# A triangular solve beside the DeltaNet groups: issue order of its second half, and later stores of its blocks

## The chip, the cores and the metric

The kernel runs on one core of a Trainium2 chip. The metric is the device time of one execution in microseconds. Every time below is of that kind or comes from one execution taken by the hardware profiler.

## The reference

One decoder layer for 512 tokens and a model width of 2048, all in float32. Two branches work in parallel on the same normalised input, and a gated sum of both is projected and added to the residual. One branch is sliding-window attention. The other is a gated DeltaNet with 16 key heads and 32 value heads of 128 channels; the change is there. Its core, cut to what matters:

```python
# chunks of C = 64 tokens, N = 8 chunks, H = 32 heads
L = jnp.where(strict, jnp.einsum('bhncd,bhnsd->bhncs', k_beta, k) * decay, 0.0)
t_inv = lax.linalg.triangular_solve(eye + L, jnp.broadcast_to(eye, L.shape),
                                    left_side=True, lower=True, unit_diagonal=True)
u = t_inv @ v_beta
w = t_inv @ (k_beta * jnp.exp(g)[..., None])
...
def step(S, xs):
    v_new = u_c - w_c @ S
    o = qd_c @ S + qk_c @ v_new
    S = S * gl_c[..., None, None] + jnp.swapaxes(kd_c, -1, -2) @ v_new
    return S, o
```

So for each of 32 heads and 8 chunks a 64 x 64 unit lower triangular matrix is inverted, and a scan over chunks uses the inverses.

## The kernel before, in words

**The main stream.** Nearly all time goes into projections on TensorE. A `channel_tile` (L227) makes 128 output channels for all 512 tokens: 16 blocks of the contraction, each as three matmuls of 128x128 by 128x512 (L223, L224, L225), because weights and activations are split into a high and a low part (`split`, L50: ScalarE writes the high part on L52, VectorE the low part on L53). A weight tile of 1 MB is loaded by `load_job` (L183) into one of two `raw` buffers; each half of it is split into one of three pairs `whi`, `wlo`. A load is issued when the second half of an older tile has been split.

**How side work is woven in.** After every second block of the contraction, `channel_tile` calls `pump` (L81). A pump advances all generators in `live`, whose `yield n` means "go on after n pumps", and those in `slow`: `paced` (L72) gives a generator a budget per pump, and its `yield x` means that x of budget must have come together before its next step. So the text of the program, written out by the generators, is one long list in which the side work stands between matmuls. `drain_slow` (L120) writes out at once what is left of a generator. A compiler pass then orders each engine's list; what must stay behind what on one engine can be given by an edge. `with tc.issue_after(ins)` (L716) puts such edges: what the block issues on the engine of `ins` stands behind `ins` in that engine's list, without a wait for a result. `self.chain` (L64) is the last instruction of the latest `rsqrt` that has been written, that is of the latest norm on VectorE.

**The stages around the change** (`deltanet`, L571). First come the keys of 16 heads (`keys`, L624) between tiles of merge gates (`merge_gate`, L242). Each key head leaves its triangular blocks in DRAM (`lt_d`, `lab_d`) and has a norm of its own (L636). Then come 16 groups (`heads`, L740), one per key head, of five channel tiles each: a query tile (`queries`, L770), two value tiles (`values`, L759) and two gate tiles. Every query and value tile goes through a causal convolution (`conv`, L554): ScalarE evicts it (L558), VectorE adds three shifted products (L561), ScalarE takes a tanh (L566), VectorE multiplies (L568); then TensorE transposes it (ptq on L781, ptv on L765, both recorded on L257). `queries` also masks two decay matrices on GpSimd (L685, L686), takes their exponentials on ScalarE (L811), and reads the solved blocks (L802 to L807). `scan` (L850) then runs the four chunk pairs and ends in an output norm (L912 to L915), whose `rsqrt` becomes the new `self.chain`.

**The solve** (`solve`, L690). Only the 64 x 64 diagonal blocks are inverted; two solves of 16 heads each: solve 0 for the heads of groups 0 to 7, solve 1 for groups 8 to 15. One solve loads 128 matrices, one on each partition, into `A` (L699), scales them (L709), and takes 62 steps of two VectorE operations: an outer product into `atmp` (L717, m x n elements a partition, n = 63 - m) and an addition into `A` (L723). Both are inside `issue_after(self.chain.ins)`. Then ScalarE copies the first 64 matrices transposed, in four parts (L728), and each part is stored in `ta_d` (L729); VectorE scales `A` in place (L733), and two stores write `ts_d` (L736). `atmp` has one buffer.

**Their paces.** Solve 0 is begun with a budget of 0.7 a pump (L596) and gets 1.4 for the last three merge-gate tiles (L602); `drain_slow` (L606) writes what is left of it before the groups begin. Solve 1 is begun there with 0.45 (L607) and drained, if anything is left, before group 8 (L617).

Of the kernel before, what the change touches and what calls it, by code (L numbers as in the profile page):

```python
# [2 lines left out]

# [22 lines left out]
HD = 64  # L26
# [10 lines left out]
class Layer:  # L37
# [533 lines left out]
    def deltanet(self):  # L571
        tc, nc, a = self.tc, self.nc, self.a
        dram = self.dram
        self.lt_d = dram.tile([2, 2, 16, 4, HD, HD], F32, name="lt_d")
        self.lab_d = dram.tile([VH, HD, 4, HD], F32, name="lab_d")
        self.ta_d = dram.tile([2, 16, 4, HD, HD], F32, name="ta_d")
        self.ts_d = dram.tile([2, 2, 16, 4, HD, HD], F32, name="ts_d")
        self.kT_d = dram.tile([KH, P, T], F32, name="kT_d")
        self.k_d = dram.tile([KH, P, T], F32, name="k_d")
        self.o_d = dram.tile([VH, P, T], F32, name="o_d")  # L580
        with ExitStack() as ps:
            self.pmm = ps.enter_context(tc.tile_pool(name="pmm", bufs=2, space=PSUM, reuse_waits="tile"))
            self.ptp = ps.enter_context(tc.tile_pool(name="ptp", bufs=2, space=PSUM, reuse_waits="tile"))
            self.gwk = ps.enter_context(tc.tile_pool(name="gwk", bufs=1, reuse_waits="tile"))
            sol1 = ps.enter_context(tc.tile_pool(name="sol1", bufs=1, side="right", reuse_waits="tile"))
            with ExitStack() as sa:
                wk = sa.enter_context(tc.tile_pool(name="dnA", bufs=2, reuse_waits="tile"))
                sol0 = sa.enter_context(tc.tile_pool(name="sol0", bufs=1, reuse_waits="tile"))
                gp = sa.enter_context(tc.tile_pool(name="gates", bufs=1, reuse_waits="tile"))
                self.go(self.gates(gp), 1)  # L590
                self.keys_done = []
                for g in range(NST):
                    self.go(self.keys(wk, g, self.acc_k[g]), 10 + 8 * g)
                for j in range(NFIRST):
                    self.merge_gate("mb", j, self.mb_d)
                s0 = self.paced(self.solve(sol0, 0, nc.vector), 0.7)  # L596
                for kind, j in self.mixed():
                    if kind == "k":
                        self.go(self.keys(wk, j, self.channel_tile(f"k{j}")), 0)
                    else:  # L600
                        self.merge_gate("mb", j, self.mb_d)
                s0[1] = 1.4  # L602
                for j in range(3):
                    self.merge_gate("ma", j, self.ma_d)
                self.drain_live()
                self.drain_slow(s0)  # L606
                s1 = self.paced(self.solve(sol1, 1, nc.vector), 0.45)  # L607
            with ExitStack() as sb:
                wk = sb.enter_context(tc.tile_pool(name="dnB", bufs=2, reuse_waits="tile"))
                self.tt = []  # L610
                for n in range(4):
                    t = wk.tile([P, NTB, P], F32, tag=f"tt{n}", name=f"tt{n}", bufs=1)
                    nc.gpsimd.memset(t[HD:P, :, 0:HD], 0.0)
                    self.tt.append(t)
                for g in range(KH):
                    if g == 8:
                        self.drain_slow(s1)  # L617
                    self.heads(wk, g)
                for j in range(3, 5):
                    self.merge_gate("ma", j, self.ma_d)  # L620
                self.drain_live()
        self.dump("o", self.o_d)
# [67 lines left out]
    def solve(self, wk, b, eng):  # L690

        nc = self.nc
        while not all(g in self.keys_done for g in range(8 * b, 8 * b + 8)):
            yield 1.0
        A = wk.tile([P, HD, HD], F32, tag=f"A{b}", name="A", bufs=1)
        bet = wk.tile([P, HD], F32, tag=f"bet{b}", name="bet", bufs=1)
        for k2 in range(2):
            s = slice(k2 * HD, (k2 + 1) * HD)
            nc.sync.dma_start(  # L699
                out=A[s].rearrange("u j i -> u (j i)"), in_=self.lt_d[b, k2].rearrange("h c j i -> (h c) (j i)")  # L700
            )
            nc.sync.dma_start(
                out=bet[s],
                in_=self.b_rows.rearrange("h (c k i) -> k (h c) i", c=4, k=2)[k2, b * HD : (b + 1) * HD, :],
            )
        yield 8.0
        nb = wk.tile([P, HD], F32, tag=f"nbet{b}", name="nbet", bufs=1)
        eng.tensor_scalar(out=nb, in0=bet, scalar1=-1.0, scalar2=None, op0=ALU.mult)
        eng.tensor_tensor(out=A, in0=A, in1=nb.unsqueeze(1).to_broadcast([P, HD, HD]), op=ALU.mult)  # L709
        eng.memset(A.rearrange("u j i -> u (j i)")[:, 0 : HD * HD : HD + 1], 1.0)  # L710
        for m in range(1, HD - 1):
            n = HD - 1 - m
            yield 0.2 + 0.0023 * m * n
            tmp = wk.tile([P, 1024], F32, tag=f"atmp{b}", name="atmp", bufs=1)
            t = tmp[:, : m * n].rearrange("p (j i) -> p j i", j=m)
            with self.tc.issue_after(self.chain.ins):  # L716
                eng.tensor_tensor(  # L717
                    out=t,
                    in0=A[:, m : m + 1, m + 1 :].to_broadcast([P, m, n]),
                    in1=A[:, :m, m : m + 1].to_broadcast([P, m, n]),  # L720
                    op=ALU.mult,
                )
                eng.tensor_tensor(out=A[:, :m, m + 1 :], in0=A[:, :m, m + 1 :], in1=t, op=ALU.add)  # L723
        for q in range(4):
            yield 1.5
            tmp = wk.tile([P, 1024], F32, tag=f"atmp{b}", name="atmp", bufs=1)
            t = tmp.rearrange("p (i j) -> p i j", j=HD)[:HD]
            nc.scalar.copy(out=t, in_=A[:HD, :, q * 16 : (q + 1) * 16].rearrange("u j i -> u i j"))  # L728
            nc.sync.dma_start(  # L729
                out=self.ta_d[b].rearrange("h c i j -> (h c) (i j)")[:, q * 1024 : (q + 1) * 1024], in_=tmp[:HD]  # L730
            )
        yield 4.5
        eng.tensor_tensor(out=A, in0=A, in1=bet.unsqueeze(2).to_broadcast([P, HD, HD]), op=ALU.mult)  # L733
        for k2 in range(2):
            s = slice(k2 * HD, (k2 + 1) * HD)
            nc.sync.dma_start(  # L736
                out=self.ts_d[b, k2].rearrange("h c j i -> (h c) (j i)"), in_=A[s].rearrange("u j i -> u (j i)")
            )
# [780 lines left out]
```

## Time and profile before

| | us |
|---|---|
| median of three runs | 2983.45 |
| lowest and highest of them | 2979.93, 2987.34 |
| the profiled execution | 2983.62 |
| its span, first to last instruction | 2981.8 |

| engine in the profiled execution | busy us | share of the span |
|---|---|---|
| TensorE | 2891.9 | 97% |
| VectorE | 1790.1 | 60% |
| ScalarE | 1085.9 | 36% |
| GpSimd | 243.0 | 8% |

The mean granted TensorE clock of that execution was 0.987. In its profile, PE is TensorE's matmuls, PEld its weight loads, DVE VectorE, ACT ScalarE, POOL GpSimd, and SP the engine that issues the DMAs here. Times in the profile count from the start of the span. A row of a stretch gives its bounds and length, and then the busy time of each engine with its number of instructions. A row in order of time gives start, length, engine, line, operation, output, inputs and shape, and in brackets how long the engine sat idle before it and what ended that. A row of waits gives the waiting instruction, what it waited for, the total in us, the number of waits and the longest.

### The profile page before, as it was taken

How to read it: one execution, taken by the hardware profiler on the slowest of the kernel's cores; microseconds unless marked ns; L12 is line 12 of the kernel's file. 1: busy time of each engine (PE TensorE's matmuls, PEld its weight loads, DVE VectorE, ACT ScalarE, POOL GpSimd, SP SyncE). 2: the span in 40 equal slices, each digit the busy share in tenths (PEclk: the TensorE clock that was granted, in tenths of full speed). 3: DMA queues.
4: the chain of work that ended last, by engine and by line, in shares of the span. 5: the costliest groups of instructions: out<-in, count | busy, mean ns of one | idle time of the engine just before them, and what ended most of it. 6: DMA issues, size and time to landing. Idle time of an engine off the chain costs nothing.

```text
span 2981.8 us, 38024 instructions
## 1 busy us (share of the span) xinstructions
PE 2891.9 (97%) x14556; PEld 2367.8 (79%) x14556; DVE 1790.1 (60%) x2903; ACT 1085.9 (36%) x2105; POOL 243.0 (8%) x204
## 2 busy tenths in 40 slices
PE   8899999999999999999999999999999999999988
PEld 6687777778787788888888878888788788788877
DVE  7755979567676544545454453433756655554697
ACT  4354332433333433333433322311334444432343
POOL 0022210111111000001100000000100000000013
PEclk9999999999999999999999999999999999999999
DMA  9756545633333533334332575555322223375562
GB/s 387 269 168 182 181 136 158 180 113 121 108 107 107 147 124 119 116 116 132 117 120 100 174 265 208 186 169 165 109 87 87 89 87 102 112 258 173 177 197 96
DMA packets 174023, 451.11 MB, mean 151 GB/s; under 512 B 72177, under 2 KB 74737, under 8 KB 138129
## 3 DMA queue, kind: packets, MB, share of 16 engines
q1 hardware_dynamic: 173842, 448.70, 45.6%
q8 instruction: 114, 1.87, 0.3%
q14 instruction: 67, 0.55, 0.1%
HBM read 386.95 MB, written 59.45 MB: 150 GB/s over the span
## 4 chain that ended last, share of the span: by engine, by line
PE 78%; DVE 9%; DMA 6%; ACT 3%; issue 2%; POOL 2%; SPq 1%; POOLq 0%; DVEq 0%; ACTq 0%
PE mm L223 22%; PE mm L225 21%; PE mm L224 21%; DVE wlo L53 2%; DMA E<-g_rows 2%; DVE wa L396 1%; PE S L1159 1%; PE pv L870 1%; ACT whi L52 1%; PE po L889 1%; PE O L1210 1%; PE pP L257 1%; DMA oraw<-o_d 1%; POOL E L685 1%; PE po L888 1%
## 5 line engine op out<-in xcount | busy, mean ns | idle before, releaser
L223 PE MATMUL mm<-hh,whi 128*128 128x512 f32 x2784 | 1138.3, 409 | 4.4 <-DVE yq L561 3.6
L225 PE MATMUL mm<-hh,wlo 128*128 128x512 f32 x2784 | 1095.5, 393 | 0.0
L224 PE MATMUL mm<-hl,whi 128*128 128x512 f32 x2784 | 1093.5, 393 | 0.0
L53 DVE TENSOR_TENSOR wlo<-raw,whi 128x1024 fp32r<-128x1024 f32 (+1 forms) x452 | 551.8, 1223 | 481.2 <-ACT whi L52 470.3
L52 ACT CAST whi<-raw 128x1024 fp32r<-128x1024 f32 (+1 forms) x452 | 470.8, 1043 | 981.9 <-PE mm L224 928.3
L223 PEld LDWEIGHTS mm<-hh,whi 128*128 128x128 f32 x2784 | 528.0, 190 | 114.9 <-issue 12.4
L225 PEld LDWEIGHTS mm<-hh,wlo 128*128 128x128 f32 x2784 | 526.6, 189 | 115.2
L224 PEld LDWEIGHTS mm<-hl,whi 128*128 128x128 f32 x2784 | 528.4, 190 | 99.8 <-issue 0.4
L223 PE MATMUL mm<-oh,whi 128*128 128x512 f32 x512 | 201.3, 395 | 2.2 <-ACT oh L52 1.2
L225 PE MATMUL mm<-oh,wlo 128*128 128x512 f32 x512 | 200.1, 391 | 0.5 <-DVE wlo L53 0.5
L224 PE MATMUL mm<-ol,whi 128*128 128x512 f32 x512 | 200.0, 391 | 0.5 <-DVE ol L53 0.5
L817 POOL TENSOR_TENSOR qe<-qe,yq 128x512 f32<-128x512 f32 x32 | 49.4, 1561 | 919.9 <-DMA qe<-eg_rows 738.9
L223 PEld LDWEIGHTS mm<-oh,whi 128*128 128x128 f32 x512 | 96.4, 189 | 24.8 <-ACT oh L52 2.6
L685 POOL TENSOR_TENSOR E<-E,neg_g 128x512 f32<-128x512 f32 x64 | 74.2, 1160 | 491.9 <-DMA E<-g_rows 465.2
L224 PEld LDWEIGHTS mm<-ol,whi 128*128 128x128 f32 x512 | 96.4, 188 | 22.3 <-DVE ol L53 1.5
L225 PEld LDWEIGHTS mm<-oh,wlo 128*128 128x128 f32 x512 | 96.5, 189 | 21.2 <-DVE wlo L53 1.3
L723 DVE TENSOR_TENSOR A<-A,atmp 128x486 f32<-128x486 f32 (+30 forms) x124 | 111.5, 905 | 1.8
L717 DVE TENSOR_TENSOR atmp<-A 128x62 f32<-128x62 f32 (+30 forms) x124 | 108.7, 882 | 1.8
L863 DVE SCALAR_TENSOR_TENSOR r<-pp,neg_eg,vt 128x128 f32<-128x128 f32 x96 | 29.3, 346 | 87.7 <-PE pp L860 85.8
L561 DVE SCALAR_TENSOR_TENSOR yv<-mm,convh,yv 128x511 f32<-128x511 f32 (+2 forms) x96 | 71.1, 741 | 8.5 <-ACT yv L558 7.5
L1183 ACT ACTIVATE sm<-sm,mx,rs 128x256 f32<-128x256 f32 (+1 forms) x128 | 71.7, 561 | 3.3 <-DVE mx L1178 3.3
L224 PE MATMUL m<-wlo,hh 128*128 128x512 f32 x128 | 51.4, 402 | 9.1 <-DVE wlo L53 9.1
(331 smaller groups left out, 3161.6 us busy)
## 6 DMA issues: line engine op xcount, KB each, us to landing
raw<-in_w_ch SPq DMA_DIRECT2D x158, 1024.0 KB
wa<-in_w_ada_ss SPq DMA_DIRECT2D x32, 1024.0 KB
raw<-in_w_od SPq DMA_DIRECT2D x32, 1024.0 KB
E<-g_rows SPq DMA_DIRECT2D x64, 256.0 KB
gw<-in_w_ada_gate SPq DMA_DIRECT2D x16, 1024.0 KB
raw<-in_w_os SPq DMA_DIRECT2D x16, 1024.0 KB
qe<-eg_rows SPq DMA_DIRECT2D x32, 256.0 KB
o_d<-zh SPq DMA_DIRECT2D x32, 256.0 KB
```

The source lines that it names most:

```text
L52: self.nc.scalar.copy(out=hi, in_=src)
L53: self.nc.vector.tensor_tensor(out=lo, in0=src, in1=hi.bitcast(F32), op=ALU.subtract)
L223: nc.tensor.matmul(ps, lhsT=wh, rhs=xh, start=first, stop=False)
L224: nc.tensor.matmul(ps, lhsT=wh, rhs=xl, start=False, stop=False)
L225: nc.tensor.matmul(ps, lhsT=wl, rhs=xh, start=False, stop=last)
L257: self.nc.tensor.transpose(dst[:, c * P : (c + 1) * P], src_cols(c), self.ident)
L561: nc.vector.scalar_tensor_tensor(out=y[:, s:], in0=ps[:, : T - s], scalar=w[:, j : j + 1], in1=y[:, s:], op0=ALU.mult, op1=ALU.add)
L685: nc.gpsimd.tensor_tensor(out=E, in0=E, in1=ng, op=ALU.add)
L717: eng.tensor_tensor(out=t, in0=A[:, m : m + 1, m + 1 :].to_broadcast([P, m, n]), in1=A[:, :m, m : m + 1].to_broadcast([P, m, n]), op=ALU.mult,
L723: eng.tensor_tensor(out=A[:, :m, m + 1 :], in0=A[:, :m, m + 1 :], in1=t, op=ALU.add)
L817: nc.gpsimd.tensor_tensor(out=qf, in0=qf, in1=q, op=ALU.mult)
L1183: nc.scalar.activation(t, t, AF.Exp, scale=r[:, h : h + 1], bias=mx[:, h : h + 1], accum_out=den[:, h : h + 1])
```

## The change

Three things differ. The edge to the latest norm is put for solve 0 alone; for solve 1 `nullcontext` takes its place. In the solve's end, the stores stand some steps of the pace behind the operations that make their data: 2.5 between a copy and its store, and 8.0 between the last scaling and the `ts_d` stores, while the yield ahead of that scaling goes from 4.5 to 1.5. And the budgets are larger: 1.9 in place of 1.4 for solve 0's last part, 0.5 in place of 0.45 for solve 1. With the yields added up, a solve asks for 15 more of budget than before (126.7 to 141.7 in all).

```diff
-                s0[1] = 1.4
+                s0[1] = 1.9
                 for j in range(3):
                     self.merge_gate("ma", j, self.ma_d)
                 self.drain_live()
                 self.drain_slow(s0)
-                s1 = self.paced(self.solve(sol1, 1, nc.vector), 0.45)
+                s1 = self.paced(self.solve(sol1, 1, nc.vector), 0.5)
...
             t = tmp[:, : m * n].rearrange("p (j i) -> p j i", j=m)
-            with self.tc.issue_after(self.chain.ins):
+            with self.tc.issue_after(self.chain.ins) if b == 0 else nullcontext():
                 eng.tensor_tensor(
...
+        rows = self.ta_d[b].rearrange("h c i j -> (h c) (i j)")
         for q in range(4):
             yield 1.5
             tmp = wk.tile([P, 1024], F32, tag=f"atmp{b}", name="atmp", bufs=1)
             t = tmp.rearrange("p (i j) -> p i j", j=HD)[:HD]
             nc.scalar.copy(out=t, in_=A[:HD, :, q * 16 : (q + 1) * 16].rearrange("u j i -> u i j"))
-            nc.sync.dma_start(
-                out=self.ta_d[b].rearrange("h c i j -> (h c) (i j)")[:, q * 1024 : (q + 1) * 1024], in_=tmp[:HD]
-            )
-        yield 4.5
+            yield 2.5
+            nc.sync.dma_start(out=rows[:, q * 1024 : (q + 1) * 1024], in_=tmp[:HD])
+        yield 1.5
         eng.tensor_tensor(out=A, in0=A, in1=bet.unsqueeze(2).to_broadcast([P, HD, HD]), op=ALU.mult)
+        yield 8.0
         for k2 in range(2):
```

More of the change, by code (lines that the diff above doesn't have):

```diff
@@ L1 @@
 import math
-from contextlib import ExitStack
+from contextlib import ExitStack, nullcontext
 import concourse.bass as bass
```

## The prediction

> **What bounds the kernel now.** I read the page's first part, then busy time by stretches cut at the DeltaNet groups, then TensorE's waits in the same stretches, then the instructions around one wait, in order of time.
>
> ```profile
> span 2981.8 us, 38024 instructions
> PE 2891.9 (97%) x14556; PEld 2367.8 (79%) x14556; DVE 1790.1 (60%) x2903; ACT 1085.9 (36%) x2105; POOL 243.0 (8%) x204
> ```
>
> TensorE is busy for 97% of the span. None of its work changes, so the edit can only give or take TensorE idle time, and the half-speed clock that follows idling. The second solve runs beside the DeltaNet groups. I cut the stretches where L912 opens a group's output norm, once in every group. Columns: PE, PEld, DVE, ACT, POOL busy (instructions), granted clock, DMA share, GB/s.
>
> ```profile
> 541.00:640.70 99.70, 93.14 (x451) 76.52 (x450) 42.86 (x58) 35.81 (x65) 10.86 (x10) 0.95 0.54 154
> 640.70:711.10 70.40, 67.54 (x358) 55.99 (x357) 51.67 (x82) 25.13 (x58) 8.05 (x6) 1.00 0.36 114
> 711.10:782.60 71.50, 69.04 (x357) 57.22 (x357) 49.62 (x77) 25.01 (x56) 7.83 (x6) 0.98 0.34 112
> 782.60:854.70 72.10, 69.11 (x358) 57.24 (x357) 49.18 (x77) 25.03 (x57) 7.77 (x6) 0.98 0.34 111
> 854.70:926.30 71.60, 69.10 (x358) 57.24 (x357) 51.30 (x80) 25.04 (x57) 7.89 (x6) 0.98 0.33 109
> 926.30:998.70 72.40, 68.69 (x357) 56.94 (x356) 51.83 (x89) 24.99 (x56) 7.99 (x6) 0.98 0.34 113
> 998.70:1070.60 71.90, 69.26 (x358) 57.20 (x357) 42.25 (x73) 32.68 (x62) 7.26 (x6) 0.98 0.54 155
> 1070.60:1137.90 67.30, 67.30 (x357) 56.02 (x357) 33.49 (x64) 25.11 (x57) 6.29 (x6) 1.00 0.37 119
> ```
>
> A period without the solve takes 67.3 us with no TensorE idle (last row). The six periods with it take 70.4 to 72.4, together 1070.6 - 640.7 = 429.9. The excess is 429.9 - 6 x 67.3 = **26.1 us**, 4.35 a period. In the row 782.6, for instance, idle is 72.10 - 69.11 = 2.99 and the clock of 0.98 costs 2% of 72, 1.4: together 4.4 of its 4.8. The first row has 99.70 - 93.14 = 6.56 idle and 5% of clock, about 5.0: 11.6 us. The waits, for 641 to 1071 (first two rows) and 541 to 641 (last two):
>
> ```profile
> PE ptv L257 <- DVE yv L568: 14.8, 6, 3.7
> PE pu L835 <- DVE Y L831: 2.3, 1, 2.3
> ...
> PE mm L223 <- DVE yq L561: 3.6, 1, 3.6
> PE ptq L257 <- DVE yq L568: 2.9, 1, 2.9
> ```
>
> So there is **one wait in each group**: the transpose of a value tile (ptv) waits for that tile's last convolution step, L568. Here is its cause, first in a group with the solve and then, from 1146, in one without.
>
> ```profile
> 650.62 0.64 POOL L686 TENSOR_SCALAR_AFFINE_SELECT E<-E 128x512 f32<-128x512 f32 x1
> 651.29 0.63 ACT L811 ACTIVATE E<-E 128x512 f32<-128x512 f32 x1 [6.25 <-POOL E L686]
> 653.60 0.63 ACT L811 ACTIVATE E<-E 128x512 f32<-128x512 f32 x1 [1.68 <-POOL E L686]
> 655.07 0.62 ACT L566 ACTIVATE th<-yv 128x512 f32<-128x512 f32 x1
> ...
> 1147.17 0.63 ACT L811 ACTIVATE E<-E 128x512 f32<-128x512 f32 x1 [4.97 <-POOL E L686]
> 1147.71 0.62 ACT L566 ACTIVATE th<-yv 128x512 f32<-128x512 f32 x1
> 1148.89 0.63 ACT L811 ACTIVATE E<-E 128x512 f32<-128x512 f32 x1 [0.57 <-POOL E L686]
> ```
>
> ScalarE runs its list in order. Without the solve, the tanh L566 stands between the two exponentials L811. With it, solve steps delay the three L561 of the convolution, L566 has slipped behind the second L811, and that one waits for a late POOL mask.
>
> **The change, part by part.** First I ask where the second solve's steps run now. L717 and L723 are the two halves of a step; here are their own busy times.
>
> ```profile
> 505.00:541.00 36.00, 12.76 (x26) 1.00 0.34 118
> 541.00:640.70 99.70, 0.00 (x0) 0.95 0.54 154
> 640.70:711.10 70.40, 9.82 (x9) 1.00 0.36 114
> ...
> sum 632.90, DVE 59.07; mean DVE 6.56
> ...
> 505.00:541.00 36.00, 13.46 (x26) 1.00 0.34 118
> ...
> 640.70:711.10 70.40, 9.15 (x9) 1.00 0.36 114
> ...
> sum 632.90, DVE 62.90; mean DVE 6.99
> ```
>
> ```profile
> 539.28 0.88 DVE L717 TENSOR_TENSOR atmp<-A 128x686 f32<-128x686 f32 x1
> 561.40 0.68 ACT L558 ACTIVATE yq<-mm,convh 128x512 f32<-128x512 f32 x1
> 643.23 0.90 DVE L717 TENSOR_TENSOR atmp<-A 128x720 f32<-128x720 f32 x1
> ```
>
> Step 14 (686 elements, 14 x 49) ran at 539, before TensorE had finished even the first tile of group 0 (its eviction is the row at 561). In the program it is written much later: at 0.45 a pump and 8 + 0.2 x 14 + 0.0023 x 5600 = 23.7 of yields it comes after 53 pumps, more than six tiles into the groups. So the compiled order follows readiness, not the place in the text. Step 15 (720 elements) is the first that was written after group 0's norm, and it runs at 643, just behind that norm. Hence the edge of `issue_after` is all that holds steps 15 to 62 back. Each group's share, 9 steps in the first, then starts right behind the norm, ahead of the convolution of the next value tile: the sensitive place.
>
> 1. **The edge goes for solve 1.** Steps 15 to 62 fill VectorE's gaps from about 541 on. Their DVE time is 59.07 - 12.76 + 62.90 - 13.46 = 95.8 us. The gaps are 99.70 - 42.86 = 56.8 us in the first stretch. In the next, the group's own DVE work is 51.67 - 9.82 - 9.15 = 32.7 of 67.3, so 34.6 are free. That makes 91.4, and the last 4 us fall into group 2, ending near 720 when packed tightly and near 760 at three quarters. No step is added, removed or resized.
>
> 2. **What goes.** All six slow periods fall to 67.3 except where the packed stretch reaches: -26.1 us. The wait for pu in the period from 998.7 goes too (it is in that sum), since group 8 finds its blocks stored long before.
>
> 3. **What comes.** The packed stretch touches groups 0, 1 and the front of 2, where VectorE has no idle time to catch up. For its price the nearest row is the bunch, which fills VectorE in the same way for some 35 us: one wait of 4.35 us. Three sensitive places (one a group) make 13.0. The second half of group 1, where the scan ran free of solve steps so far, can cost nothing (the scan's steps wait for TensorE, and steps of 1 us fit between) or another wait, 4.35; I take half, 2.2. The lower bound for the whole stretch comes from solve 0 beside the keys:
>
> ```profile
> 150.00:303.00 153.00, 147.04 (x713) 121.42 (x712) 87.22 (x189) 73.65 (x188) 34.41 (x36) 0.98 0.59 179
> 303.00:541.00 238.00, 225.55 (x1009) 185.13 (x1009) 215.11 (x309) 85.68 (x166) 32.83 (x32) 0.96 0.50 155
> ```
>
> There VectorE is 90% busy, and idle plus clock is 12.45 + 9.5 = 22 us in 238, against 5.96 + 3.1 = 9 in 153, or 14 in 238, without the solve: about 8 us of loss for a whole solve. So the stretch costs 8 at the low end, 15.2 as I take it, and 39 at the high end (the second rival).
>
> 4. **The stores and the pace.** Solve 0 ends with this:
>
> ```profile
> 550.14 4.42 DVE L733 TENSOR_TENSOR A<-A,bet 128x4096 f32<-128x4096 f32 x1 [2.90 <-ACT atmp L728]
> ...
> 555.78 14.78 DMA raw<-in_w_ch
> ```
>
> L733 holds VectorE for 4.42 us and delays the split behind it; the two 1 MB stores of ts_d go out first, the weight load then takes 14.78, and TensorE waits in the first stretch (3.6 and 2.9). The new yields write the stores later, but by the evidence above a store still goes when its block is ready, and SP has little else to issue then. I take 0; if the load does get ahead of the stores, up to the stretch's 11.6 us is won. The tail of solve 1 (four copies, L733, 2 MB of stores) moves from 1012 to 1035 into group 2 or 3. There it costs 0 (at 1030 TensorE waited for no weights) to 11.6; I take 0, the row of this same tail. The paces 1.9 and 0.5 only change where steps are written: 0.
>
> **Sum**: -26.1 + 13.0 + 2.2 = -10.9 us. The profiled execution took 2983.62 (span 2981.8 and 1.8 around it), 0.17 above the median of 2983.45. Forecast: **2972.6 us**.
>
> The Trainium skill, "SBUF — State Buffer", section "Who interferes with whom", speaks against the change: a VectorE instruction with two SBUF inputs shuts out a GpSimd instruction that reads SBUF for its whole length, and the other way round. Here are the first mask operation of a pair with the solve and without, which agree with it (2.03 against 1.05 us):
>
> ```profile
> 648.52 2.03 POOL L685 TENSOR_TENSOR E<-E,neg_g 128x512 f32<-128x512 f32 x1
> ...
> 1145.38 1.05 POOL L685 TENSOR_TENSOR E<-E,neg_g 128x512 f32<-128x512 f32 x1
> ```
>
> By that rule every mask in the packed stretch may be late, which would move the sum towards the second rival below.
>
> **Rivals.**
>
> - *The stretch is cheap, or the load gets ahead of the stores.* At solve 0's price: -26.1 + 8 = -18.1, 2965.4; with the load ahead as well, 2953.8. For it: solve 0's rows. Against: beside the keys no scan and no query chain runs.
> - *Slower: the stretch never recovers.* Gaps are packed to three quarters, so 95.8 us of steps spread over groups 0, 1 and 2, and each of their nine convolution tiles (a query and two values a group) holds TensorE as the first does now: 9 x 4.35 = 39.2, so +13.1, 2996.6. It decides from the seventh wait on (6 x 4.35 = 26.1 breaks even). For it: POOL's lengthened masks and the ScalarE order above. Against: in a bunch only one tile of the three waits, and beside the keys it was less.
> - *Nothing moves*: the steps stay near their places in the text, or as many waits come as go: 2983.5. Against it stands step 14 at 539.
>
> **How the numbers follow.** Chances: the forecast 0.45 (its own range 2967 to 2980: no second wait in group 1, or one or two more), cheap 0.20, nothing 0.19, slower 0.16. About 0.3%, 9 us, is what can be told from no change, so faster means under 2974.5 and slower over 2992.4. Faster gets 0.30 of the forecast and 0.20: 0.50. Slower gets 0.13 of its rival. Same is the rest, 0.37. The range 2962 to 2992 leaves out the load ahead of the stores (0.07) and most of the slower rival (0.13).
>
> **What would show it.** Right: L717 runs without a break from 512 to between 720 and 760; the periods from the third or fourth group on are 67.3 us with the clock at 1.00; the ptv waits after 641 fall from six to two or three, and pu's goes. Wrong: L717 still in bunches behind L912 (nothing moves); more than six TensorE waits between 541 and 780 (slower); a TensorE wait for raw weights where solve 1's stores now lie (tail mis-sized); the 14.78 us load gone (stores mis-sized).

## The result and the profile after

| | before | after |
|---|---|---|
| median of four runs each on one chip, us | 2983.61 | 2968.06 |
| lowest and highest | 2979.93, 2987.34 | 2966.22, 2968.59 |
| the profiled execution | 2983.62 | 2968.14 |
| its span | 2981.8 | 2964.4 |

The ratio is 0.9945, with a 95% interval of 0.9932 to 0.9957: 15.5 us faster by the medians.

Busy time by stretches of the kernel after comes first, cut where a group's output norm opens (L913 in this kernel). From L729 to the end of `solve`, and below it, its lines are one or more higher than in the kernel before.

```profile
541.00:639.30 98.30, 92.06 (x453) 76.09 (x452) 92.94 (x106) 36.68 (x66) 13.72 (x10) 0.97 0.53 154
639.30:711.80 72.50, 68.81 (x358) 57.28 (x357) 69.02 (x111) 25.11 (x57) 7.62 (x6) 0.98 0.35 111
711.80:786.50 74.70, 70.59 (x358) 58.12 (x357) 39.40 (x66) 32.69 (x62) 7.60 (x6) 0.95 0.51 150
786.50:853.80 67.30, 67.30 (x357) 56.03 (x356) 33.50 (x64) 25.11 (x57) 5.88 (x6) 1.00 0.38 118
```

Four of the six long periods are gone. Two are left: 72.5 and 74.7, together 147.2 - 134.6 = 12.6 us above two periods of 67.3. Before, the six held 26.1. The stretch ahead of the first norm lost 6.56 us of TensorE idle and 5% of clock before, and loses 6.24 and 3% now.

The second solve's outer products, L717 alone, in the same execution:

```profile
505.00:541.00 36.00, 13.08 (x26) 1.00 0.38 121
541.00:639.30 98.30, 27.72 (x24) 0.97 0.53 154
639.30:711.80 72.50, 18.36 (x24) 0.98 0.35 111
```

They are spread over two stretches and, as the trace shows, finished by 711.9, so VectorE is busy for 92.94 of 98.30 us and then for 69.02 of 72.50. TensorE's waits from 541 to 1056 (us in total, times, longest):

```profile
PE mm L223 <- DVE yq L561: 6.2, 1, 6.2
PE pto L257 <- DVE osb L920: 3.7, 1, 3.7
PE pu L836 <- DMA lab<-lab_d: 2.8, 1, 2.8
PE ptv L257 <- DVE yv L568: 1.3, 1, 1.3
```

All but one of the six waits for a value tile (ptv) have gone; the one that is left is 1.3 us long, where the longest was 3.7. The other three in this list each have a cause of their own, read here one after the other.

**A norm pulled apart (group 1, 3.7 us).** VectorE in order of time, before and then after, from the opening of group 0's norm to the multiplication of `osb` that TensorE waits for:

```profile
640.74 0.16 DVE L912 SCALAR_TENSOR_TENSOR ms<-osq,epsq 128x4 f32<-128x4 f32 x1 [2.67 <-ACT junk L893]
...
643.14 0.17 DVE L64 SCALAR_TENSOR_TENSOR roy<-rot,roy 128x8 f32<-128x8 f32 x1
...
644.05 1.29 DVE L919 TENSOR_TENSOR osb<-osb,roy 128x512 f32<-128x512 f32 x2
```

```profile
639.34 0.16 DVE L913 SCALAR_TENSOR_TENSOR ms<-osq,epsq 128x4 f32<-128x4 f32 x1
639.42 1.13 DVE L717 TENSOR_TENSOR atmp<-A 128x936 f32<-128x936 f32 x1
640.47 0.16 DVE L913 SCALAR_TENSOR_TENSOR ms<-osq,epsq 128x4 f32<-128x4 f32 x1
...
654.37 0.16 DVE L64 SCALAR_TENSOR_TENSOR roy<-rot,roy 128x8 f32<-128x8 f32 x1
654.44 1.09 DVE L723 TENSOR_TENSOR A<-A,atmp 128x902 f32<-128x902 f32 x1
655.45 1.29 DVE L920 TENSOR_TENSOR osb<-osb,roy 128x512 f32<-128x512 f32 x2
```

The norm is a chain of instructions of 0.16 us, each of which needs the one before. Before, its only solve step is the L717 at 643.23, behind the last link, and it takes 3.3 us from its opening to `osb`. Now a solve step or a step of the main stream stands between nearly all of its links, and it takes 16.1 us.

**The tail of solve 1 on ScalarE (group 2, 2.8 us).** The profile puts this wait down to a load of `lab`. But `py`, the product that reads `lab`, ran at 731.79, so that load, issued at 734.74 and 736.04, is already the next group's. What `pu` needs is `Y`. TensorE, then VectorE, then ScalarE in order of time:

```profile
731.79 0.68 PE L830 MATMUL py<-ta,lab 64*64 64x64 f32 x16
738.23 0.36 PE L836 MATMUL pu<-tt,Y 64*64 64x64 f32 x1 [2.81 <-DMA lab<-lab_d]
```

```profile
734.11 0.75 DVE L561 SCALAR_TENSOR_TENSOR yv<-mm,convh,yv 128x511 f32<-128x511 f32 x1 [6.33 <-ACT yv L558]
...
737.76 0.41 DVE L832 COPY Y<-py 128x256 f32<-128x256 f32 x1
```

```profile
731.50 1.99 ACT L729 COPY atmp<-A 64x1024 f32<-64x1024 f32 x1 [2.78 <-DMA ta_d<-atmp]
733.40 0.68 ACT L558 ACTIVATE yv<-mm,convh 128x512 f32<-128x512 f32 x1
```

`Y` ends at 738.17 and `pu` begins at 738.23. VectorE had been idle for 6.33 us ahead of the first L561 of the value tile, and `Y` stands behind it. That L561 waits for the tile's eviction L558, which stands on ScalarE behind a copy of solve 1's tail; and the copy waits until the store before it has read the single `atmp` buffer. One group later, where no copy stands in the way, L558 begins 2.8 us ahead of `py` (802.03 against 804.85) and `Y` ends 1.5 us behind it; here L558 begins 1.6 us behind `py` and `Y` ends 6.4 behind it. The kernel before has the same chain at 1017 to 1024, where it costs the 2.3 us of pu that the prediction quotes. So this wait has not gone. It has moved with the solve's end.

This wait cost more than its length. Stretches ahead of it, right behind it and later; the third number from the right is the granted clock:

```profile
728.00:735.30 7.30, 7.30 (x49) 5.70 (x48) 1.19 (x2) 4.25 (x5) 0.00 (x0) 1.00 0.72 214
738.30:744.20 5.90, 5.90 (x27) 4.73 (x28) 5.90 (x5) 2.01 (x3) 0.00 (x0) 0.50 0.26 56
745.00:752.00 7.00, 7.00 (x36) 5.84 (x35) 2.86 (x5) 3.08 (x5) 0.00 (x0) 1.00 0.92 204
```

**Convolution steps torn apart (group 0, 6.2 us).** VectorE after TensorE's second tile of group 0 in the kernel after; ScalarE had begun to evict the query tile at 561.74:

```profile
567.77 1.10 DVE L717 TENSOR_TENSOR atmp<-A 128x902 f32<-128x902 f32 x1
568.79 0.74 DVE L561 SCALAR_TENSOR_TENSOR yq<-mm,convh,yq 128x511 f32<-128x511 f32 x1
569.45 1.09 DVE L723 TENSOR_TENSOR A<-A,atmp 128x902 f32<-128x902 f32 x1
570.46 0.74 DVE L561 SCALAR_TENSOR_TENSOR yq<-mm,convh,yq 128x510 f32<-128x510 f32 x1
...
571.77 0.74 DVE L561 SCALAR_TENSOR_TENSOR yq<-mm,convh,yq 128x509 f32<-128x509 f32 x1
```

The three L561 read the tile where the matmuls left it, in a PSUM buffer. The third ends at 572.51; the first matmul of the third tile waits for it and starts at 572.66. Solve steps keep the first L561 back until 568.79, and a solve step and an L561 of the value tile (in the line left out) stand between the three.

The span after is shorter by 17.4 us: 1.4 at the opening of group 0's norm (640.74 to 639.34), 13.5 in the groups, and 2.5 behind the groups, where nothing was changed. The execution's time around the span is 3.7 us in place of 1.8, so that 15.5 are left.

### The profile page after: what moved, and what is told of

It is laid out like the page before. It is cut to its first block, busy times and chain, and to the rows that moved or that the text cites. A ratio compares the mean times of both kernels' runs of the same rounds, so it can differ in the third digit from the quotient of the medians.

```text
span 2964.4 us, 38028 instructions
## 1 busy us (share of the span) xinstructions
PE 2882.8 (97%) x14556; PEld 2362.5 (80%) x14556; DVE 1786.1 (60%) x2903; ACT 1086.6 (37%) x2105; POOL 236.2 (8%) x204
## 4 chain that ended last, share of the span: by engine, by line
PE 81%; DVE 9%; DMA 4%; ACT 2%; issue 2%; POOL 1%; SPq 0%; POOLq 0%; DVEq 0%; ACTq 0%
PE mm L223 23%; PE mm L225 22%; PE mm L224 22%; DVE wlo L53 2%; DMA E<-g_rows 1%; DVE wa L396 1%; PE S L1160 1%; PE po L890 1%; PE pv L871 1%; PE O L1211 1%; DVE A L723 1%; PE pP L257 1%; DVE atmp L717 1%; ACT whi L52 1%; PE pd L886 1%
## 5 line engine op out<-in xcount | busy, mean ns | idle before, releaser
L53 DVE TENSOR_TENSOR wlo<-raw,whi 128x1024 fp32r<-128x1024 f32 (+1 forms) x452 | 548.6, 1216 | 491.6 <-ACT whi L52 476.6
L52 ACT CAST whi<-raw 128x1024 fp32r<-128x1024 f32 (+1 forms) x452 | 470.8, 1043 | 951.7 <-PE mm L224 907.0
L685 POOL TENSOR_TENSOR E<-E,neg_g 128x512 f32<-128x512 f32 x64 | 76.6, 1197 | 490.9 <-DMA E<-g_rows 427.7
L717 DVE TENSOR_TENSOR atmp<-A 128x392 f32<-128x392 f32 (+30 forms) x124 | 108.1, 877 | 2.0
L723 DVE TENSOR_TENSOR A<-A,atmp 128x392 f32<-128x392 f32 (+30 forms) x124 | 108.0, 876 | 2.0
L561 DVE SCALAR_TENSOR_TENSOR yv<-mm,convh,yv 128x511 f32<-128x511 f32 (+2 forms) x96 | 71.3, 743 | 8.2 <-ACT yv L558 6.8
```

Of the source, the lines that this page charges most:

```text
L52: self.nc.scalar.copy(out=hi, in_=src)
L53: self.nc.vector.tensor_tensor(out=lo, in0=src, in1=hi.bitcast(F32), op=ALU.subtract)
L561: nc.vector.scalar_tensor_tensor(out=y[:, s:], in0=ps[:, : T - s], scalar=w[:, j : j + 1], in1=y[:, s:], op0=ALU.mult, op1=ALU.add)
L685: nc.gpsimd.tensor_tensor(out=E, in0=E, in1=ng, op=ALU.add)
L717: eng.tensor_tensor(out=t, in0=A[:, m : m + 1, m + 1 :].to_broadcast([P, m, n]), in1=A[:, :m, m : m + 1].to_broadcast([P, m, n]), op=ALU.mult,
```

## The experiments

A stretch's loss is worked out as TensorE's idle time plus the part of the clock that was not granted, from the rows of each profile; for the periods it is their time above 67.31. "Group 0" is the stretch from 541 to the opening of its norm. Clocks are read to two digits, so a loss there is good to half a microsecond. Each profile is of one execution, and executions of one kernel differ in time by up to 16 us, so two losses that are a few us apart say little by themselves.

| kernel | loss in group 0, us | loss in the periods with the solve, us | median, us | ratio (95%) |
|---|---|---|---|---|
| before | 11.6 | 26.0 | 2983 to 2985 | 1 |
| after | 9.2 | 12.5 | 2968.06 | 0.9945 (0.9932 to 0.9957) |
| e1, the edge alone | 14.4 | 11.3 | 2972.28 | 0.9956 (0.9941 to 0.9971) |
| e2, stores and paces | 0.9 | 23.2 | 2968.46 | 0.9954 (0.9938 to 0.9971) |
| e5, solve 0's pace | 1.2 | 27.4 | 2974.46 | 0.9967 (0.9953 to 0.998) |
| e6, the stores | 11.1 | 24.9 | 2980.48 | 1.0 (0.9987 to 1.0013) |
| e13, solve 1's pace | 10.7 | 19.2 | 2981.95 | 0.9987 (0.9976 to 0.9998) |
| e3, before, solve 1 behind a value tile | 0.5 | 2.4 | 2953.61 | 0.9894 (0.9879 to 0.9909) |
| e4, before, exponentials behind the tanh | 11.7 | 9.4 | 2972.5 | 0.9956 (0.994 to 0.9973) |
| e8, after, solve 1 behind a value tile | 0.8 | 1.0 | 2948.83 | 0.9894 (0.9879 to 0.9909) |
| e9, e8 and e4 together | 0 | 1.0 | 2947.71 | 0.9891 (0.9876 to 0.9906) |
| e11, after, exponentials behind the tanh | 9.0 | 12.0 | 2969.02 | 0.9948 (0.9936 to 0.9961) |
| e12, after, free behind group 0's value tile | 0 | 11.9 | 2967.51 | 0.9937 (0.9921 to 0.9952) |

Each ratio is against runs of the kernel before on the same chip: medians 2985.47 for e1 to e4, 2982.62 for e5 to e9, 2984.59 for e11 to e13.

**e1: the edge alone.**

```diff
-            with self.tc.issue_after(self.chain.ins):
+            with self.tc.issue_after(self.chain.ins) if b == 0 else nullcontext():
```

> The kernel before with the edge taken from solve 1 alone; stores and paces as before. Theory (the edge is the whole change): 2968 us, ratio 0.9948, with the groups' periods at 67.3 from the third on. Rival (the later stores or the paces carry part of it): over 2973 us.

Measured: 2972.28, ratio 0.9956, between the two forecasts; the periods from the third on take 67.3. The periods lose 11.3 instead of 26.0, with a wait of pto and one of pu. Pu waits for `Y` here too, but behind another step of the tail: the last copy begins at 728.76 and L558 at 732.14, and what stands ahead of `Y` on VectorE (738.95) is L733, for 4.43 us from 730.84. Group 0 loses 14.4, where before it lost 11.6. TensorE's waits from 541 to 1056, the first two:

```profile
PE mm L223 <- DVE yq L561: 8.3, 1, 8.3
PE pto L257 <- DVE osb L919: 4.1, 1, 4.1
```

So the free edge brings both waits, and neither needs the other parts of the change.

**e2: the rest of the change, with the edge kept.** The paces 1.9 and 0.5 and the later stores, as in the diff.

> The kernel before with the later stores and the larger paces alone; the edge stays for both solves. Theory: 2983.5 us, within 3 us of before, the same wait for L568 in each of six groups. Rival (stores get behind the weight load): group 0 gains up to 11 us, 2972 us.

Measured: 2968.46, ratio 0.9954, as fast as the whole change. That was not to be had from the periods, which still lose 23.2 (five long ones in place of six). It comes from group 0, which loses 0.9 in place of 11.6:

```profile
561.13 2.31 DVE L561 SCALAR_TENSOR_TENSOR yq<-mm,convh,yq 128x511 f32<-128x511 f32 x3
```

The query tile's three L561 run back to back in this kernel (one row, x3). Before, they stand in turn with those of the value tile behind it:

```profile
562.68 0.74 DVE L561 SCALAR_TENSOR_TENSOR yq<-mm,convh,yq 128x511 f32<-128x511 f32 x1
566.84 0.75 DVE L561 SCALAR_TENSOR_TENSOR yv<-mm,convh,yv 128x511 f32<-128x511 f32 x1 [3.41 <-ACT yv L558]
567.50 0.74 DVE L561 SCALAR_TENSOR_TENSOR yq<-mm,convh,yq 128x510 f32<-128x510 f32 x1
```

VectorE waits 3.41 us for the eviction of the value tile, with two steps of the query tile behind it, and the query tile's PSUM buffer comes free that much later. This is the first stretch's wait of 3.6 before. It isn't the weight load.

**e5, e6, e13: which part of e2.** Each is the kernel before with one of the three edits: `s0[1] = 1.9`; the three yields of the stores; the pace 0.5 for solve 1.

> The kernel before with 1.9 in place of 1.4 for solve 0's last part, and nothing else. The run with stores and paces alone won 11 us in group 0. Theory (solve 0's last steps, written sooner, come sooner in VectorE's list, and its tail clears group 0's first tiles): that group falls by 10 us, about 2973 us. Rival (it was the later stores, or solve 1's pace): 2983 us.

> The kernel before with the later stores alone (the yields 2.5, 1.5 and 8.0), both paces as before. Theory: a store still goes when its block is ready, so nothing, 2983 us. Rival (the weight load gets ahead of the 1 MB stores): group 0 falls by 10 us, 2973 us.

> The kernel before with only the second solve's pace at 0.5 a pump in place of 0.45. Theory 1 (with the edge in place, a group takes as many steps as are written in it): the solve ends one group earlier, one of the six long periods goes, and the time falls by 3 to 6 us, 2977 to 2981. Theory 2 (the pace only shows where steps are written; the readiness of the operands sets the rest): six long periods as before, and the time is within 2 us of the kernel before, 2981 to 2985.

Measured: 2974.46 for solve 0's pace, 2980.48 with a ratio of 1.0 for the stores, 2981.95 for solve 1's pace. The stretches from 541 to the first norm, with the pace (first) and with the stores:

```profile
541.00:628.50 87.50, 86.28 (x437) 71.52 (x436) 43.07 (x57) 33.66 (x64) 12.38 (x10) 1.00 0.61 173
```

```profile
541.00:642.30 101.30, 95.22 (x460) 78.26 (x460) 44.90 (x61) 37.76 (x68) 10.89 (x10) 0.95 0.53 152
```

Solve 0's pace alone takes away group 0's loss; it leaves six long periods. The later stores move nothing that can be told from no change. Solve 1's pace saves one long period (19.2 of loss in place of 26.0), but its median fell by only 2.6, less than the 3 to 6 expected and less than its profile shows.

In all the kernels here, group 0's wait goes with VectorE's order: where the query tile's L561 stand together (e2, e3, e5, e8, e9, e12), TensorE loses 0 to 1.2 us; where the value tile's (before, e4, e6, e13) or solve steps (after, e1, e11) stand between them, 9 to 14. Why solve 0's pace makes the compiler choose the one order and not the other, no run shows; e3 has the good order with the old pace.

**e3: solve 1 put behind a chosen place.** The edge is kept, but its anchor is the last convolution step of each group's second value tile instead of the latest norm.

```diff
-        nc.vector.scalar_tensor_tensor(out=y, in0=th, scalar=1.0, in1=y, op0=ALU.add, op1=ALU.mult)
+        self.conv_end = nc.vector.scalar_tensor_tensor(out=y, in0=th, scalar=1.0, in1=y, op0=ALU.add, op1=ALU.mult)
...
-            with self.tc.issue_after(self.chain.ins):
+            with self.tc.issue_after((self.anchor if b and self.anchor else self.chain).ins):
...
         yield from self.conv(wk, ps, 32 + 2 * g + e, y)
+        if e:
+            self.anchor = self.conv_end
```

> The kernel before, but solve 1's steps are queued behind the last convolution step of the second value tile of each group, not behind the output norm: the same number of steps a group, in a bunch just as dense, at another place. Theory of the sensitive place (a bunch costs only where it meets the first value tile): the ptv waits go, periods 67.3 to 68.5, about 2960 us, less than after. Rival (any bunch that fills VectorE costs a wait of 4 us a group): 2983 us as before.

Measured: 2953.61, ratio 0.9894, nearly twice the gain of the change. By the table, 23.6 us of it come from the periods, where the steps were moved, and 11 from group 0, where the L561 of the query tile stand together. Stretches of this kernel:

```profile
541.00:632.00 91.00, 90.54 (x454) 74.73 (x453) 59.69 (x80) 35.75 (x67) 11.85 (x10) 1.00 0.57 166
632.00:699.30 67.30, 67.30 (x357) 56.02 (x356) 49.46 (x80) 25.11 (x57) 6.20 (x6) 1.00 0.37 118
...
901.20:970.90 69.70, 67.84 (x357) 55.91 (x357) 51.02 (x91) 32.75 (x61) 5.83 (x6) 1.00 0.45 134
```

In the second row VectorE does the same work as in the long period from 640.7 before (49.46 us in 80 instructions against 51.67 in 82), and TensorE never waits. The solve costs nothing in this group; its place behind the norm cost 4.35 on the mean of the six.

**e4: the order on ScalarE.** In the kernel before, both exponentials L811 are held behind the tanh of the group's first value tile.

```diff
-        nc.scalar.activation(th, y, AF.Tanh)
+        self.tanh[t] = nc.scalar.activation(th, y, AF.Tanh)
...
-        for e in range(2):
-            nc.scalar.activation(M[e], M[e], AF.Exp)
+        with self.tc.issue_after(self.tanh[32 + 2 * g].ins):
+            for e in range(2):
+                nc.scalar.activation(M[e], M[e], AF.Exp)
```

> The kernel before, with one edge on ScalarE: the two exponentials L811 of a group stand behind the tanh L566 of its first value tile. VectorE's order rules are untouched. Theory (TensorE waits because the tanh slipped behind the exponentials, and those wait for POOL's masks): most of the ptv waits go, the excess of 26 us falls to 10 or less, about 2966 us. Rival (the value tile is late on VectorE itself): the waits shrink by less than a third, over 2975 us.

Measured: 2972.5, ratio 0.9956. ScalarE's order in group 1 (lines stand one or two higher here), and TensorE's waits for ptv from 541 to 1056:

```profile
656.25 0.63 ACT L567 ACTIVATE th<-yv 128x512 f32<-128x512 f32 x1 [1.66 <-DVE yv L562]
656.79 1.14 ACT L813 ACTIVATE E<-E 128x512 f32<-128x512 f32 x2
```

```profile
PE ptv L258 <- DVE yv L569: 4.2, 4, 1.7
```

The waits for ptv fall from 14.8 to 4.2 us and the periods' loss from 26.0 to 9.4, with the solve's steps still behind the norm. So most of each bunch's price was the tanh behind a late mask. Of what is left, 3.9 us are in the period of pu's wait; in the row above the tanh still waits 1.66 us for VectorE's L562, ahead of which a solve step and a split stand. The time is 6 us above the 2966 that was expected.

**e8 and e9: the place and the change together.** e8 is the kernel after with e3's anchor; e9 has e4's edge as well.

> The changed kernel with solve 1 queued behind each group's second value tile in place of no edge. Theory: as with the old stores and paces, groups at 67.3 and no wait in group 0; solve 1 ends in group 6, so its tail is as cheap as there or cheaper: 2950 to 2954 us. Rival (the later stores carry a cost of their own): 2957 us or more.

> The same with the two exponentials behind the first value tile's tanh as well. Theory: once the steps run behind the value tiles, the exponentials wait for nothing that matters, so nothing more is won: within 3 us of the run without it. Rival: the order on ScalarE still costs something in the groups, and 3 us or more are won.

Measured: 2948.83 and 2947.71, ratios 0.9894 and 0.9891. Beside e3 that is no difference in the ratio, and the edge on ScalarE adds nothing where no step stands ahead of a tanh. Both beat the kernel before and the kernel after.

**e11: the kernel after with the exponentials behind the tanh.** The edge of e4 in the kernel after.

> The kernel after, with both exponentials L812 of a group held behind the tanh L566 of its first value tile on ScalarE. Theory 1 (what is left of the loss in groups 1 and 2 is the output norm of group 0 drawn out between solve steps, and the loads of the inverse blocks behind a store of the second solve): the exponentials have no part in either wait, the periods of groups 0 and 1 stay at 72 to 75 us, and the time is that of the kernel after within 4 us, 2964 to 2972. Theory 2 (the late exponentials cost the packed stretch as they cost the bunches): the two long periods fall to 68 to 70 us and the time to 2956 to 2961.

Measured: 2969.02, 2966.15 to 2972.7: the time of the kernel after. Its waits from 541 to 1056:

```profile
PE mm L224 <- DVE yq L562: 6.0, 1, 6.0
PE pto L258 <- DVE osb L922: 3.5, 1, 3.5
PE pu L838 <- DVE Y L834: 2.5, 1, 2.5
```

The ptv wait of 1.3 us is gone, but the two periods lose 12.0 us as against 12.5: the late exponentials had no part in the rest, so on that Theory 1 holds. Its last clause does not: `pu` waits for `Y` here by the profile too, not for the blocks' loads. It is the chain over ScalarE that was read above in the kernel after: a copy at 733.41, L558's counterpart at 735.34, `Y` at 738.79.

**e12: free, but only behind group 0's second value tile.** The kernel after, with e3's edge and an anchor that is set once.

```diff
         yield from self.conv(wk, ps, 32 + 2 * g + e, y)
+        if e and not g:
+            self.anchor = self.conv_end
```

> The kernel after, with the second solve held behind the last convolution step L568 of group 0's second value tile, and free from there on. Theory 1 (the free edge costs some 10 us in group 0, where solve steps stand between the convolution steps L561 that free the buffers, and 12.5 in the groups behind it, where they draw out the output norm): group 0's norm opens at 628 to 632 and not at 639, the two or three periods behind it still lose 8 to 15 us together with a wait of pto for osb, and the time is 2956 to 2962. Theory 2 (the loss of group 0 only moves: VectorE is full for as long as 48 steps have to pass, wherever they begin): group 0 wins 8 to 10 us and the periods behind it lose as much more, 20 us and up, and the time is 2966 to 2972.

Measured: the median of 2967.51 lies in Theory 2's range, but the profile goes with Theory 1: group 0 loses nothing, and the groups behind it lose 11.9 us, no more than after.

```profile
541.00:629.80 88.80, 88.80 (x449) 73.61 (x448) 70.89 (x89) 33.91 (x67) 11.88 (x10) 1.00 0.59 169
629.80:700.20 70.40, 67.05 (x356) 55.66 (x355) 68.79 (x97) 24.80 (x55) 7.72 (x6) 1.00 0.35 113
```

```profile
PE pto L258 <- DVE osb L923: 6.5, 2, 3.4
PE pu L839 <- DMA lab<-lab_d: 3.8, 1, 3.8
```

Two norms are now pulled apart instead of one (two waits of pto), and pu's wait is there again, with the same chain behind it (a copy at 789.88 ahead of L558's counterpart at 791.83, `Y` at 796.19). The profiled execution took 2960.26, as Theory 1 has it; the five runs lie between 2960.26 and 2970.89, and what the longer ones lost, no profile shows. That part stays open.

## Why the prediction was right, and where not

**The time** was forecast at 2972.6 and came out at 2968.06, inside the range; the mechanism of the periods was the right one, several terms were not.

- **Which work moves, and when it ends: right.** L717 runs without a break from 513 and ends at 712, a little ahead of the 720 to 760 forecast. From the third period on, 67.3 us at full clock. Ptv's waits fell from six to one, where two or three were forecast.
- **What goes, -26.1: right in its cause, and in all but pu's wait.** That wait was counted as gone, with nearly all of its period's 4.54 (ptv waits only 0.3 us there, and 3.9 of that period stay in e4 where the others shrink), and it came back in group 2. e3 moves the same steps past the value tiles, with 2.4 us left of 26.0, and e4 takes the tanh out from behind the masks, with 9.4 left.
- **What comes, +15.2: the size about right, the waits others.** 4.35 of the sum was for group 0, and 10.9 for the periods, where 12.5 came. I priced it as ptv waits of 4.35 behind late masks. The ptv wait is 1.3 in all, in group 2, where no solve step runs any more. What came is the norm pulled apart, which costs 72.51 - 67.31 = 5.2, and the tail of solve 1, which is most of the 74.62 - 67.31 = 7.3 in the next one (pu's wait of 2.8 and 5% of the clock, 3.7 by the rounded figure; the ptv wait of 1.3 is the rest). A wait for `osb` stands in the four kernels in which solve steps run free of an edge past a norm (after, e1, e11, e12) and in no other; no run keeps them out of the norm alone. I had read the edge only as the thing that puts the bunch in a bad place; that it also keeps the norm's chain whole, I didn't see.
- **Group 0: wrong in its reason.** I gave the stretch one more wait (4.35) and blamed its old loss on the 14.78 us weight load behind the stores. The 3.6 of that loss is the order of the L561 (e2, e5); only the ptq wait of 2.9 goes back to the load by the trace, where the split L52 waits for it (570.63) and the tanh stands behind that split (571.58). No run takes the load alone away. The free edge put solve steps into the same place, and the loss stayed: 11.6 before, 9.2 after.
- **Step 4, stores 0: right** within the interval of e6, 0.9987 to 1.0013. **Paces 0: wrong.** The step failed with "the paces only change where steps are written". A changed place in the text is a changed order in the compiled list, and solve 0's pace alone takes group 0's loss from 11.6 to 1.2 us (e5); solve 1's pace takes away one long period (e13).
- **The tail of solve 1, taken as 0: wrong.** I took the row of the same tail at 1014 to 1035 for one that costs nothing, since no weights were waited for. Its price stood in another row, pu's 2.3, which I had put down to stores and loads of the blocks. In seven kernels (before, after, e4, e5, e6, e11, e12) a copy stands ahead of L558 and pu waits 1.9 to 3.8 us; in e1 it is L733. In e2, e3, e8, e9 and e13 all four copies fall where no L558 stands behind them, and pu doesn't wait: the tail has its price by where it falls, as the steps have.

That the sum came so near is partly luck, since two errors worked against each other. By their ratios the edge alone wins 13 us (e1) and the rest of the change alone 14 (e2), but the whole wins 16, not 27: the free edge takes back in group 0 (0.9 of loss in e2, 9.2 after) most of what solve 0's pace had won there. Pricing the pace at nothing was wrong by about 10 us, and pricing the free edge at 4.35 in group 0 was wrong by some 4 the other way. Where the forecast had -15.2 in the periods and +4.35 in group 0, -13.5 and -2.4 came.

The second rival's mechanism, all nine convolution tiles at 4.35, did not come. The Trainium skill, "SBUF — State Buffer", section "Who interferes with whom", says that VectorE's two-input instructions and GpSimd's SBUF reads shut each other out; the masks of group 2 in the kernel after agree with it:

```profile
720.91 1.50 POOL L686 TENSOR_SCALAR_AFFINE_SELECT E<-E 128x512 f32<-128x512 f32 x1
...
723.51 0.63 POOL L686 TENSOR_SCALAR_AFFINE_SELECT E<-E 128x512 f32<-128x512 f32 x1
```

The same operation takes 1.50 and 0.63 us. Beside the first, VectorE runs a split L53 with two inputs in SBUF (720.51 to 721.92), beside the second L927, one of whose inputs lies in PSUM. In the packed stretch the masks ran long too (2.01 us for an L685 at 590.90, 1.46 for an L686 at 649.36), and no ptv waited there.

## What to carry to other kernels

Here the side work on an engine with idle time cost by its place, not by its length: with an edge, put such work behind the last instruction on which the bound engine will wait, as in e3, rather than behind whatever came last or nowhere. Before an edge is removed, ask what it protects: a serial chain of short instructions can be pulled apart by filler that is ready (3.3 to 16.1 us here). Where two parts of a change act in one stretch, run each alone; their gains need not add up.

## What the runs showed of the hardware

A TensorE wait of 2.8 us was followed by at least 5.9 us at a granted clock of 0.50 (the stretch from 738.3 above), so that the wait cost about twice its length. The clock of 0.98 in the period with the wait of 3.7, and of 0.97 in the stretch with that of 6.2, tell the same. The length alone doesn't decide it: after e5's wait of 1.92 us at 1010.75 the trace has 3.41 us at half clock, while in the kernel before the period from 640.7, with a wait of 2.86, and in e12 the period from 629.8, with one of 3.35, keep a clock of 1.00. In all these traces the half-speed stretches from 541 to 1138 last 3.41, 6.83 or 10.24 us, one, two or three times the same length.
